# Interleaving the second FFN's up steps with the preceding group's down tiles, and using block products in 15 of its steps instead of 9

## The chip, the cores and the metric

The kernel runs on one core of one Trainium2 chip. The metric is the device time of one execution in microseconds (us). The kernel before was timed three times; its median is 1150.75 us.

## The reference

Two layers of a diffusion transformer work on 512 latent tokens of width 1024 (with 256 context tokens in the first layer). Layer 0 mixes tokens by attention, layer 1 by a Fourier transform, and each ends with a gated feed-forward network (FFN) with a width-3 convolution over the tokens. The change is in the FFN of layer 1 alone. All values are float32.

```python
def conv_ffn(h, w_up, conv_w, conv_b, w_down):     # h 512x1024, w_up 1024x5632, w_down 2816x1024
    u = h @ w_up
    up = jnp.pad(u, ((0, 0), (1, 1), (0, 0)))
    u = up[:, :-2] * conv_w[0] + up[:, 1:-1] * conv_w[1] + up[:, 2:] * conv_w[2] + conv_b
    gate, val = jnp.split(u, 2, axis=-1)
    return (jax.nn.silu(gate) * val) @ w_down

x = x + g1 * rms_norm(y, norm_g[i, 1])
h = modulate(rms_norm(x, norm_g[i, 2]), sh2, sc2)
x = x + g2 * rms_norm(conv_ffn(h, ...), norm_g[i, 3])       # g2 comes from c @ mod_w, a matrix-vector product
```

## The kernel before

Activations lie transposed in SBUF: 128 channels on the partitions, 8 chunks of channels, 512 tokens along the free axis. `xT` is the residual stream (16 KB per partition), `yT` the output of the FFN being summed up, `hh` and `hl` the FFN's input h as a high and a low part.

**Products in three parts.** Each float32 operand is split into a high and a low part, and each product is three matmuls: high by high (L99), high by low (L100), low by high (L101). A weight tile comes by DMA into a ring of three SBUF buffers named `raw` (issued on the queue SP, L131). Then `split` (L122) makes the high part `wh` by a cast on ACT (ScalarE) and the low part `wl` by a subtraction on DVE (VectorE). Both go into rings of five buffers. So each weight tile needs DVE before PE (TensorE) can run the third matmul of its first chunk. A `raw` buffer is free for the next load when the last `split` that reads it is done. Products gather in six PSUM buffers `mm`.

**Up steps.** The FFN has 22 steps, fi = 0 to 21, each for 128 gate channels and 128 value channels. Steps 0 to 2 are begun early, under the norm before the FFN. An ordinary step loads one `raw` of 1 MB (gate and value), splits two weight tiles of 128x1024, and runs 2 x 8 x 3 = 48 matmuls of 128x512. A *block step* (the steps listed in `SEVEN`) takes the same weights as a 2x2 block product by seven products (Strassen's scheme in a variant of Winograd): 7 products x 4 chunks x 3 = 84 matmuls of 128x256 instead of the equivalent of 96. For this, `seven_inputs` forms, once per layer and just ahead of step `SUMS[l]`, four sums of blocks of h on DVE (L1088 to L1091, in place in `yT`) and four more splits (`zh`, `zl`). In every block step `seven_weights` forms three sums of weight blocks on DVE (L1104, L1106, L1107) into a second `raw` buffer, and splits four weight tiles; `seven_products` then runs the seven products, with PSUM copies on ACT and two additions on DVE (L1146, L1149).

**After each step**: the convolution (ACT L1200, DVE L1201 and L1203 for each half), SiLU (ACT L1213), the gating product (DVE L1214), and a split of the gated tile into `xh`, `xl`.

**Groups and down tiles.** The 22 steps are cut into groups of 8, 6 and 8. After a group come 8 *down tiles* d = 0 to 7, one for each 128 output channels. Each loads a slice of w_down, splits it, runs 3 matmuls of 128x512 per step of the group, and copies (first group, ACT) or adds (later groups, DVE L1321) the result to `yT`. After each down tile of the first group, one piece of a matrix-vector product for g2 runs: loads of 1 MB of `in_mod_r` into `raw`, and multiply-adds on DVE (L416, L419). The last group's down tiles run for tokens 0 to 255 first, then `mid` begins the closing norm of that half, then tiles 1 to 7 for tokens 256 to 511 follow.

**What sets the order.** A scheduler places the program's instructions on each engine's list at compile time. It takes, of the instructions whose inputs its own model has ready, the one that stands earliest in the program. On the chip each engine then runs its list strictly in order, and an instruction that waits holds everything behind it. Layer 0 parks `xT` in DRAM (`away`) during its own FFN; layer 1 keeps it in SBUF.

## Time and profile before

| | us |
|---|---|
| median of 3 runs (range) | 1150.75 (1148.4 to 1152.72) |
| profiled execution, its own time | 1151.45 |
| its span in the trace | 1149.7 |
| PE busy | 1117.8 (97%) |
| DVE busy | 877.7 (76%) |
| ACT busy | 578.3 (50%) |
| FFN of layer 1, steps 3 to 7 | 805.5 to 862 |
| its eight first down tiles, with the matrix-vector product | 862 to 907 |
| its nine block steps, each | 10.2 to 10.4 |

The span runs from the first to the last instruction in the trace. Busy time of an engine is an average over stages: DVE's 76% has stretches near 100% in it. A row of a windows view gives, for a stretch of the span, the busy time of PE, PE's weight load, DVE, ACT and POOL, each with its number of instructions, then the granted PE clock (1.00 is full), the DMA engines' busy share and their GB/s. A row of a timeline view gives start, duration, engine, line of the kernel, operation, output and inputs, and in brackets the idle time before it and what ended it.

### The profile page before, as it was taken

To read this page: it belongs to the slowest core of one execution; us is meant where nothing else is said; L and a number is where in the kernel's file an instruction comes from. 1 tells how busy PE (TensorE), PEld (TensorE's weight loads), DVE (VectorE), ACT (ScalarE), POOL (GpSimd) and SP (SyncE) were. 2 spreads that over 40 slices of the span, in tenths; PEclk is the share of its full clock that TensorE was granted. 3 is DMA by queue.
4 is the path that set the end of the run, shared out by engine and by line. 5 is a ranking of instruction groups with operands and counts; after the bars stand their busy time and mean duration, and the time that the engine had idled before them with its cause. 6 is when DMAs were issued, how large, how long until landed. Compare 5 with 4: busy or idle time off the path is not lost.

```text
span 1149.7 us, 19092 instructions
## 1 busy us (share of the span) xinstructions
PE 1117.8 (97%) x7642; PEld 963.9 (84%) x7642; DVE 877.7 (76%) x1422; ACT 578.3 (50%) x1030; POOL 174.0 (15%) x178
## 2 busy tenths in 40 slices
PE   8999999999999999999999998989999999999995
PEld 4689988868888978887998898869887888899895
DVE  4678777765679976987998568988997498679745
ACT  4342356666665633552465445557743355256442
POOL 1236332521420000000000153500000000000023
PEclk9999999999999999999999999999999999999998
DMA  9576101075142355545525300630228123223212
GB/s 366 239 242 214 44 1 38 7 265 205 38 184 111 125 196 198 214 131 201 193 98 191 113 9 15 206 106 35 74 84 281 46 103 111 93 91 111 92 56 74
DMA packets 30881, 149.51 MB, mean 130 GB/s; under 512 B 3140, under 2 KB 7876, under 8 KB 18632
## 3 DMA queue, kind: packets, MB, share of 16 engines
q1 hardware_dynamic: 30792, 148.29, 36.5%
q8 instruction: 60, 0.98, 0.3%
q14 instruction: 29, 0.24, 0.1%
HBM read 144.08 MB, written 4.19 MB: 129 GB/s over the span
## 4 chain that ended last, share of the span: by engine, by line
PE 84%; DVE 8%; ACT 5%; issue 2%; POOL 1%; DMA 0%; DVEq 0%; SPq 0%; ACTq 0%; POOLq 0%
PE mm L99 24%; PE mm L100 23%; PE mm L101 23%; PE PT L914 1%; ACT wh L122 1%; PE mm L174 1%; PE O L99 1%; DVE md_t L291 1%; PE gm L492 1%; PE gm L99 1%; PE O L100 1%; PE gm L101 1%; PE gm L100 1%; PE O L101 1%; PE misc L180 1%
## 5 line engine op out<-in xcount | busy, mean ns | idle before, releaser
L122 ACT CAST wh<-raw 128x1024 fp32r<-128x1024 f32 (+2 forms) x189 | 180.5, 966 | 188.4 <-PE mm L100 128.1
L122 DVE TENSOR_TENSOR wl<-raw,wh 128x1024 fp32r<-128x1024 f32 (+3 forms) x179 | 204.2, 1148 | 63.2 <-ACT wh L122 63.1
L99 PE MATMUL mm<-hh,wh 128*128 128x256 f32 (+2 forms) x652 | 220.8, 339 | 1.4 <-ACT yT L889 0.9
L100 PE MATMUL mm<-hl,wh 128*128 128x256 f32 (+2 forms) x652 | 218.5, 335 | 0.0
L101 PE MATMUL mm<-hh,wl 128*128 128x256 f32 (+2 forms) x652 | 218.4, 335 | 0.0
L266 POOL TENSOR_TENSOR gacc<-gacc,sq 128x256 f32<-128x256 f32 (+1 forms) x35 | 29.9, 855 | 716.0 <-ACT sq L264 715.1
L99 PEld LDWEIGHTS mm<-hh,wh 128*128 128x128 f32 x652 | 122.6, 188 | 18.7 <-ACT sq L1140 2.7
L100 PEld LDWEIGHTS mm<-hl,wh 128*128 128x128 f32 x652 | 122.7, 188 | 14.1
L101 PEld LDWEIGHTS mm<-hh,wl 128*128 128x128 f32 x652 | 122.7, 188 | 14.0
L99 PE MATMUL mm<-xh,wh 128*128 128x512 f32 (+1 forms) x368 | 132.1, 359 | 0.0
L100 PE MATMUL mm<-xl,wh 128*128 128x512 f32 (+1 forms) x368 | 130.9, 356 | 0.0
L101 PE MATMUL mm<-xh,wl 128*128 128x512 f32 (+1 forms) x368 | 130.4, 355 | 0.0
L99 PE MATMUL mm<-zh,wh 128*128 128x256 f32 x304 | 87.0, 286 | 0.0
L100 PE MATMUL mm<-zl,wh 128*128 128x256 f32 x304 | 84.7, 279 | 0.0
L101 PE MATMUL mm<-zh,wl 128*128 128x256 f32 x304 | 84.5, 278 | 0.0
L99 PEld LDWEIGHTS mm<-xh,wh 128*128 128x128 f32 x368 | 69.2, 188 | 12.8 <-issue 2.1
L100 PEld LDWEIGHTS mm<-xl,wh 128*128 128x128 f32 x368 | 69.2, 188 | 11.2 <-issue 0.4
L101 PEld LDWEIGHTS mm<-xh,wl 128*128 128x128 f32 x368 | 69.2, 188 | 10.9
L1200 ACT ACTIVATE cv<-mm,cols 128x512 f32<-128x512 f32 x64 | 49.7, 777 | 26.2 <-PE mm L101 23.3
L99 PEld LDWEIGHTS mm<-zh,wh 128*128 128x128 f32 x304 | 57.2, 188 | 3.5 <-ACT sq L1143 2.7
L101 PEld LDWEIGHTS mm<-zh,wl 128*128 128x128 f32 x304 | 57.3, 188 | 0.0
L1201 DVE SCALAR_TENSOR_TENSOR cv<-mm,cols,cv 128x511 f32<-128x511 f32 x64 | 47.6, 745 | 12.6 <-ACT cv L1200 11.7
(417 smaller groups left out, 2684.8 us busy)
## 6 DMA issues: line engine op xcount, KB each, us to landing
raw<-in_w_up SPq DMA_DIRECT2D x44, 1024.0 KB, 4.9
xT<-in_mod_r SPq DMA_DIRECT2D x20, 1024.0 KB, 5.0
raw<-in_w_down SPq DMA_DIRECT2D x32, 512.0 KB, 3.7
raw<-in_mod_p SPq DMA_DIRECT2D x8, 1024.0 KB, 4.8
raw<-in_w_in SPq DMA_DIRECT2D x6, 1024.0 KB, 7.6
raw<-in_w_down SPq DMA_DIRECT2D x16, 384.0 KB, 3.1
yT<-in_mod_r SPq DMA_DIRECT2D x10, 512.0 KB, 5.9
raw<-in_w_out SPq DMA_DIRECT2D x4, 1024.0 KB, 5.0
```

The lines of the kernel that those rows point to most:

```text
L99: i = PE.matmul(out, lhsT=ah, rhs=bh, start=start, stop=False, skip_group_check=skip)
L100: PE.matmul(out, lhsT=ah, rhs=bl, start=False, stop=False, skip_group_check=skip)
L101: return i, PE.matmul(out, lhsT=al, rhs=bh, start=False, stop=stop, skip_group_check=skip)
L122: i = S.copy(out=h, in_=src), eng.tensor_tensor(out=l, in0=src, in1=f(h), op=ALU.subtract)
L174: PE.matmul(ps[:32, :src.shape[1]], lhsT=ones32, rhs=src, start=True, stop=True)
L180: PE.matmul(ps[32 * j:32 * j + 32, :w], lhsT=ones32, rhs=sq[:, j * w:(j + 1) * w], start=first, stop=last)
L266: G.tensor_tensor(out=self.acc[:, sl], in0=self.acc[:, sl], in1=sq[:, sl], op=ALU.add)
L291: m = V.scalar_tensor_tensor(out=t, in0=yT[:, k, hs], scalar=der[:, l, gi, k:k + 1], in1=R, op0=ALU.mult, op1=ALU.mult)
L492: PE.matmul(ps[32 * q:32 * q + 32, :], lhsT=spad[:, k, :], rhs=w[:, q * T:(q + 1) * T], start=k == 0, stop=k == KC - 1)
L914: PE.transpose(out=pt[:, j * P:(j + 1) * P], in_=Ps[j][:, off:off + P], identity=ident)
L1200: S.activation(out=cv, in_=ps, func=AF.Identity, bias=bc, scale=wc[1])
L1201: V.scalar_tensor_tensor(out=cv[:, 1:], in0=ps[:, :T - 1], scalar=wc[0], in1=cv[:, 1:], op0=ALU.mult, op1=ALU.add)
```

## The change

In layer 1 only:

- the groups become 4, 6, 6, 6 steps; `SUMS` goes from 7 to 6 and `SEVEN` from nine steps to all of 7 to 21;
- the down tiles of a group (all but the last group's) become a generator that is advanced after up steps of the next group, by the table `DOWN`: after step 7 two tiles, after 8 and 9 three each, after 10 to 12 one each, and so on; the matrix-vector product for g2 goes with the tiles of the first group, so with steps 7 to 9;
- `xT` is written to DRAM after the norm ahead of the FFN; its SBUF holds the gated tiles of steps 0 to 3 and 10 to 13; it is loaded back ahead of the last group's down tiles;
- the down weights become one array for each layer and group.

The seven products, the splits and the convolution are as before. Lines move by two to three (L122 becomes L124, L1088 to L1091 become L1090 to L1093, L1104 becomes L1106, L1201 and L1203 become L1204 and L1206, L1214 becomes L1217, L419 becomes L421).

```diff
-GROUPS = [(0, 8), (8, 6), (14, 8)]
+GROUPS = [[(0, 8), (8, 6), (14, 8)], [(0, 4), (4, 6), (10, 6), (16, 6)]]
-SUMS = [5, 7]
-SEVEN = [(5, 6, 8, 10, 12, 14, 15, 17, 18, 20), (8, 9, 11, 12, 14, 15, 17, 18, 20)]
+SUMS = [5, 6]
+SEVEN = [(5, 6, 8, 10, 12, 14, 15, 17, 18, 20), (7, 8, 9, 10, 11, 12, 13, 14, 15, 16, 17, 18, 19, 20, 21)]
+DOWN = {7: 2, 8: 3, 9: 3, 10: 1, 11: 1, 12: 1, 13: 2, 14: 1, 15: 2, 16: 1, 17: 1, 18: 1, 19: 2, 20: 1, 21: 2}
...
-                gs["t"] = xp.pair([P, 2, T])
+                gs["t"] = places.pop(0) if l and (f0 == 0 or f0 == 10 and fi < 14) else xp.pair([P, 2, T])
...
+        def down_part(gi, w, g_, d, hs, ps=None, end=False):
+            ps, sl = y_mm(pps, w, g_, hs, True, ps)
+            if gi == 0:
+                S.copy(out=yT[:, d, sl], in_=ps[:, sl])
+            else:
+                V.tensor_tensor(out=yT[:, d, sl], in0=yT[:, d, sl], in1=ps[:, sl], op=ALU.add)
+            if end:
+                ys.add(pps, yT[:, d, sl], hs)
+
+        def down_weights(gi, nch, d, pairs):
+            r = raw([P, nch, P], a["w_down%d%d" % (l, gi)][d])
+            wh, wl = pairs([P, nch, P])
+            split(wh, wl, r)
+            return [(wh[:, c, :], wl[:, c, :]) for c in range(nch)]
+
+        def down_tiles(gi, nch, g_):
+            yield
+            for d in range(KC):
+                down_part(gi, down_weights(gi, nch, d, wpair), g_, d, [0, 1])
+                pump(gem, GP[1])
+                yield
...
             remod(1, *n2, R[1], eng=V)
+            SY.dma_start(out=away, in_=xT)
+            xp2 = mk(cp, [P, 2, 2, 2, T], F32R, "xT")
+            places = [(xp2[:, i, 0], xp2[:, i, 1]) for i in (0, 1, 0, 1)]
...
-        for gi, (f0, nch) in enumerate(GROUPS):
+        down = iter(())
+        for gi, (f0, nch) in enumerate(GROUPS[l]):
...
                 gated(fi, cc[0], cc[1], f0)
...
+                if l:
+                    pump(down, DOWN.get(fi, 0))
+            pump(down, 100)
+            if l and end:
+                xT = mk(cp, [P, KC, T], F32, "xT")
+                SY.dma_start(out=xT, in_=away)
             g_ = [gs[fi] for fi in range(f0, f0 + nch)]
+            if l and not end:
+                down = down_tiles(gi, nch, g_)
+                pump(down)
+                continue
```

The scheduler's lists move with this. Three places follow; a name's numbers tell one use of a buffer from the next.

**DVE, steps 5 to 7 of layer 1, before.** `wl_1300` is the value half's weights of step 5, `wl_1305` and `wl_1309` the gate's and the value's of step 6, `wl_1324` the gate's of step 7; `cv` is the convolution; L1088 is the first of the four input sums.

```order
L122 TENSOR_TENSOR wl_1300_8961<-raw_1294_8925,wh_1299_8960 128x1024
L1214 TENSOR_TENSOR cv1_1291_8915<-cv0_1287_8882,cv1_1291_8915 128x512
L122 TENSOR_TENSOR wl_1305_9000<-raw_1303_8997,wh_1304_8999 128x1024
L122 TENSOR_TENSOR xl_1293_8922<-cv1_1291_8915,xh_1292_8921 128x512
L1201 SCALAR_TENSOR_TENSOR cv0_1298_8956<-mm_1297_8931,cols_2_64,cv0_1298_8956 128x511
L122 TENSOR_TENSOR wl_1309_9033<-raw_1303_8997,wh_1308_9032 128x1024
L1203 SCALAR_TENSOR_TENSOR cv0_1298_8956<-mm_1297_8931,cols_2_64,cv0_1298_8956 128x511
L1088 TENSOR_TENSOR yT_5_68<-yT_5_68 128x4x256
L122 TENSOR_TENSOR wl_1324_9094<-raw_1322_9091,wh_1323_9093 128x1024
```

The same place in the change, in two pieces of which the second goes on where the first ends. `wl_1297` is the value half's weights of step 5, L1090 and L1091 are the first two input sums.

```order
L124 TENSOR_TENSOR wl_1297_8959<-raw_1291_8923,wh_1296_8958 128x1024
L1217 TENSOR_TENSOR cv1_1288_8913<-cv0_1284_8880,cv1_1288_8913 128x512
L1204 SCALAR_TENSOR_TENSOR cv0_1295_8954<-mm_1294_8929,cols_2_64,cv0_1295_8954 128x511
L1090 TENSOR_TENSOR yT_5_68<-yT_5_68 128x4x256
L124 TENSOR_TENSOR xl_1290_8920<-cv1_1288_8913,xh_1289_8919 128x512
L1206 SCALAR_TENSOR_TENSOR cv0_1295_8954<-mm_1294_8929,cols_2_64,cv0_1295_8954 128x511
```

The rows right behind them: `zl` are the input blocks' low parts, L1092 and L1093 the other two sums, and `wl_1310` is the gate's weights of step 6.

```order
L1091 TENSOR_TENSOR yT_5_68<-yT_5_68 128x4x256
L124 TENSOR_TENSOR zl_1301_9000<-yT_5_68,zh_1300_8999 128x1024
L1204 SCALAR_TENSOR_TENSOR cv1_1299_8987<-mm_1298_8962,cols_2_64,cv1_1299_8987 128x511
L1092 SCALAR_TENSOR_TENSOR yT_5_68<-yT_5_68 128x4x256
L1206 SCALAR_TENSOR_TENSOR cv1_1299_8987<-mm_1298_8962,cols_2_64,cv1_1299_8987 128x511
L1093 SCALAR_TENSOR_TENSOR yT_5_68<-yT_5_68 128x4x256
L1217 TENSOR_TENSOR cv1_1299_8987<-cv0_1295_8954,cv1_1299_8987 128x512
L124 TENSOR_TENSOR zl_1303_9004<-yT_5_68,zh_1302_9003 128x1024
L124 TENSOR_TENSOR xl_1290_8920<-cv1_1299_8987,xh_1289_8919 128x512
L124 TENSOR_TENSOR zl_1305_9008<-yT_5_68,zh_1304_9007 128x1024
L124 TENSOR_TENSOR zl_1307_9012<-yT_5_68,zh_1306_9011 128x1024
L124 TENSOR_TENSOR wl_1310_9018<-raw_1308_9015,wh_1309_9017 128x1024
```

Before, one instruction stands between step 5's value weights and step 6's gate weights; in the change sixteen do, the whole of the input sums and their splits among them.

**PE, from the last matmul of step 5 on, before.** `mm_1301` is step 5's value product, `mm_1306` step 6's gate product.

```order
L101 MATMUL mm_1301_8964<-hh_6_69,wl_1300_8961 128x512
L100 MATMUL mm_1306_9003<-hl_7_70,wh_1304_8999 128x512
L101 MATMUL mm_1306_9003<-hh_6_69,wl_1305_9000 128x512
L99 MATMUL mm_1306_9003<-hh_6_69,wh_1304_8999 128x512
L100 MATMUL mm_1306_9003<-hl_7_70,wh_1304_8999 128x512
```

The same in the change: `mm_1298` is step 5's value product, `mm_1311` and `mm_1315` step 6's gate and value products, `mm_1330` the first product of block step 7.

```order
L103 MATMUL mm_1298_8962<-hh_6_69,wl_1297_8959 128x512
L102 MATMUL mm_1311_9021<-hl_7_70,wh_1309_9017 128x512
L101 MATMUL mm_1315_9054<-hh_6_69,wh_1313_9050 128x512
L102 MATMUL mm_1315_9054<-hl_7_70,wh_1313_9050 128x512
L101 MATMUL mm_1330_9112<-hh_6_69,wh_1321_9095 128x256
L102 MATMUL mm_1330_9112<-hl_7_70,wh_1321_9095 128x256
L103 MATMUL mm_1311_9021<-hh_6_69,wl_1310_9018 128x512
```

Five matmuls that need high parts only stand ahead of the first one that reads `wl_1310`; before, step 6's second matmul already reads its `wl`.

**DVE, the matrix-vector product among the first group's down tiles, before.** L419 works on `raw` tiles loaded from `in_mod_r`; the `wl` here are down weights.

```order
L419 SCALAR_TENSOR_TENSOR gacc_1339_9223<-raw_1341_9232,scol_12_77,gacc_1339_9223 128x1024
L122 TENSOR_TENSOR xl_1313_9068<-cv1_1330_9155,xh_1312_9067 128x512
L122 TENSOR_TENSOR wl_1344_9239<-raw_1342_9236,wh_1343_9238 128x1024
L419 SCALAR_TENSOR_TENSOR gacc_1339_9223<-raw_1346_9268,scol_12_77,gacc_1339_9223 128x1024 x2
L122 TENSOR_TENSOR wl_1349_9275<-raw_1347_9272,wh_1348_9274 128x1024
L419 SCALAR_TENSOR_TENSOR gacc_1339_9223<-raw_1351_9304,scol_12_77,gacc_1339_9223 128x1024 x2
```

Part of it in the change, around the end of block step 8. `wl_1353` and `wl_1355` are the last two weight tiles of block step 8, `wl_1366` and `wl_1371` down weights, L421 the matrix-vector product on `raw_1368`, loaded from `in_mod_r`; L1148 and L1151 are the additions at the end of block step 8.

```order
L124 TENSOR_TENSOR wl_1353_9281<-raw_1347_9268,wh_1352_9280 128x1024
L124 TENSOR_TENSOR xl_1318_9086<-cv1_1334_9209,xh_1317_9085 128x512
L124 TENSOR_TENSOR wl_1355_9285<-raw_1346_9266,wh_1354_9284 128x1024
L124 TENSOR_TENSOR wl_1366_9399<-raw_1364_9396,wh_1365_9398 128x512
L421 SCALAR_TENSOR_TENSOR gacc_1339_9237<-raw_1368_9416,scol_12_77,gacc_1339_9237 128x1024
L1148 TENSOR_TENSOR mm_1356_9288<-mm_1356_9288,sq_1358_9290 128x512
L421 SCALAR_TENSOR_TENSOR gacc_1339_9237<-raw_1368_9416,scol_12_77,gacc_1339_9237 128x1024
L1151 TENSOR_TENSOR mm_1357_9289<-mm_1357_9289,sq_1359_9291 128x512
L1204 SCALAR_TENSOR_TENSOR cv0_1360_9382<-mm_1356_9288,cols_2_64,cv0_1360_9382 128x511
L124 TENSOR_TENSOR wl_1371_9423<-raw_1369_9420,wh_1370_9422 128x512
```

In the lists before, the L419 rows stand between down weights alone, behind all of step 7 and ahead of block step 8's weight sums; now they stand between the splits, additions and convolutions of block steps 7 to 9.

More of the change, by code (lines that the diff above doesn't have):

```diff
@@ L1178, in ffn @@
     def ffn(l, xp, ready, pre, mid, gem, plain=None):
+        nonlocal xT
         ys = YStat()
@@ L1296, in ffn @@
             :, :, NF:], scalar1=-1.0, scalar2=None, op0=ALU.mult)
-        for gi, (f0, nch) in enumerate(GROUPS):
-            end = gi == len(GROUPS) - 1
+        down = iter(())
+        for gi, (f0, nch) in enumerate(GROUPS[l]):
+            end = gi == len(GROUPS[l]) - 1
             for fi in range(max(f0, FIRST), f0 + nch):
@@ L1627, in _layout @@
     out = {}
-    for h, (f0, n) in enumerate(GROUPS):
-        out["w_down%d" % h] = wd[:, f0:f0 + n].transpose(0, 3, 2, 1, 4)
+    for l, groups in enumerate(GROUPS):
+        for g, (f0, n) in enumerate(groups):
+            out["w_down%d%d" % (l, g)] = wd[l, f0:f0 + n].transpose(2, 1, 0, 3)
     wf = i["fourier_w_out"][0].reshape(4, 256, D)
```

13 lines of the change are left out of this document (2 added, 11 removed).

## The prediction

> **What bounds the kernel now.** I read the page's busy shares and its chain of waits first.
>
> ```profile
> PE 1117.8 (97%) x7642; PEld 963.9 (84%) x7642; DVE 877.7 (76%) x1422; ACT 578.3 (50%) x1030; POOL 174.0 (15%) x178
> PE 84%; DVE 8%; ACT 5%; issue 2%; POOL 1%; DMA 0%; DVEq 0%; SPq 0%; ACTq 0%; POOLq 0%
> ```
>
> PE is at work in 97% of the span and carries 84% of the chain that ended last. So work taken off PE saves time one for one, and any idling of PE is lost the same way. What could make PE idle shows only stage by stage, in the windows view of layer 1's FFN (PE, PEld, DVE, ACT, POOL busy, then clock, DMA share, GB/s): steps 3 to 6, step 7 and the tail of 6, then the first group's down tiles.
>
> ```profile
> core 0: us, PE busy (x) PEld busy (x) DVE busy (x) ACT busy (x) POOL busy (x), PEclk, DMA share, GB/s
> 790.00:833.40 43.40, 43.23 (x248) 37.62 (x247) 41.60 (x86) 35.76 (x63) 0.00 (x0) 1.00 0.14 49
> 833.40:856.80 23.40, 23.40 (x103) 18.97 (x102) 22.25 (x26) 12.56 (x17) 0.00 (x0) 1.00 0.14 46
> 862.00:907.00 45.00, 45.00 (x201) 35.59 (x200) 28.82 (x30) 15.13 (x20) 0.00 (x0) 1.00 0.57 197
> ```
>
> PE is full in all three. But DVE is full as well from 790 to 857 (41.60 of 43.40 us, then 22.25 of 23.40): there it just keeps up, and nothing can be put in front of it unseen. Only in the down tiles has it air (28.82 of 45). This decides the forecast: the change spends DVE's time earlier.
>
> **The saving.** A block step against an ordinary one, by the stretches that each occupies on PE:
>
> ```profile
> 907.19:917.61 10.42, 10.42 (x86) 10.10 (x85) 3.11 (x4) 5.18 (x8) 0.00 (x0) 1.00 0.08 34
> 917.61:928.01 10.40, 10.33 (x87) 9.94 (x86) 10.13 (x14) 7.10 (x12) 0.00 (x0) 1.00 0.53 185
> 928.01:939.21 11.20, 11.20 (x51) 9.01 (x50) 10.97 (x16) 6.43 (x10) 0.00 (x0) 1.00 0.04 17
> ```
>
> The first two are block steps, the third an ordinary one of 11.20 us (48 matmuls, 0.233 us each). The nine block steps' stretches, cut like these, have a mean of 10.35 us. Six more of them save 6 x (11.20 - 10.35) = **5.1 us**.
>
> **A stall at step 6.** On DVE's list the change puts all of the input sums and their splits between step 5's last weights and step 6's first. What these cost, from the DVE timeline of before, start to start:
>
> ```profile
> 832.27 1.22 DVE L122 TENSOR_TENSOR wl<-raw,wh 128x1024 fp32r<-128x1024 f32 x1
> 833.40 0.68 DVE L1214 TENSOR_TENSOR cv<-cv,cv 128x512 f32<-128x512 f32 x1
> 834.00 1.22 DVE L122 TENSOR_TENSOR wl<-raw,wh 128x1024 fp32r<-128x1024 f32 x1
> ...
> 838.17 0.74 DVE L1203 SCALAR_TENSOR_TENSOR cv<-mm,cols,cv 128x511 f32<-128x511 f32 x1
> 838.83 1.21 DVE L1088 TENSOR_TENSOR yT<-yT 128x1024 f32<-128x1024 f32 x1
> 839.96 1.22 DVE L122 TENSOR_TENSOR wl<-raw,wh 128x1024 fp32r<-128x1024 f32 x1
> ...
> 843.55 1.21 DVE L1090 SCALAR_TENSOR_TENSOR yT<-yT 128x1024 f32<-128x1024 f32 x1
> 844.68 0.68 DVE L1214 TENSOR_TENSOR cv<-cv,cv 128x512 f32<-128x512 f32 x1
> ```
>
> So 1.13 us for anything 1024 wide (split or sum), 0.60 for a gating product or a split 512 wide, 0.66 for a tap of the convolution. The row at 832.27 is step 5's value weights; the row at 834.00 is step 6's gate weights, on time. In the change 17 instructions run from 833.40 up to and with `wl_1310`: nine of 1024 (four sums, four `zl`, itself), 10.2 us; four of 512, 2.4; four taps, 2.6; together 15.2 us. Waits on the way: the second of them needs step 5's gate product and its pass through ACT, about 0.6 us; the taps of step 5's value half wait some 0.3 for theirs. So `wl_1310` is ready near 833.4 + 15.2 + 0.9 = 849.5.
>
> PE's side, from its timeline:
>
> ```profile
> 805.54 0.50 PE L99 MATMUL mm<-hh,wh 128*128 128x512 f32 x1 [0.17 <-DVE sq L1199]
> ```
>
> This is the start of step 3. Three steps of 11.20 end at 839.1. The five matmuls that PE's list has ahead of the first use of `wl_1310` take 3 x 0.233 + 2 x 0.118 = 0.9, so PE stands at 840.1 and idles until 849.5: **9.4 us**. It is a plain loss: PE's work behind it is not shorter, and DVE's load is not less. Bounds: with no wait on DVE's side 8.5; if the value half's chain through ACT is as slow as the one which costs 0.55 more at the `xl` split between those rows, twice, 10.5.
>
> **The clock after it.** The trace has one such gap, at the end of the Fourier stage:
>
> ```profile
> 752.00:756.40 4.40, 1.06 (x18) 0.69 (x20) 3.90 (x5) 1.71 (x5) 1.47 (x1) 1.00 0.80 257
> 756.40:759.80 3.40, 3.40 (x46) 2.21 (x47) 1.70 (x7) 1.18 (x5) 0.00 (x0) 0.50 0.73 284
> 759.80:770.00 10.20, 9.59 (x89) 6.64 (x88) 9.61 (x28) 6.03 (x16) 0.00 (x0) 1.00 0.01 2
> ```
>
> PE worked 1.06 of 4.40 us, then had half its clock (0.50) for 3.4 us although it was busy throughout, then all of it. A gap of 9.4 us brings the same at least: half of 3.4 us lost, **1.7 us**; bounds 0 and 3.4 (twice the row).
>
> [...]
>
> **Steps 7 to 9 with tiles and the matrix-vector product.** Here a ring of three `raw` buffers has to hold a block step's weights, its sums, down weights, and four loads of `in_mod_r`. Landing times and the DVE work on them:
>
> ```profile
> raw<-in_w_up SPq DMA_DIRECT2D x44, 1024.0 KB, 4.9
> raw<-in_mod_r SPq DMA_DIRECT2D x4, 1024.0 KB, 5.0
> raw<-in_w_down SPq DMA_DIRECT2D x16, 384.0 KB, 3.1
> ...
> 861.80 0.75 DVE L416 TENSOR_SCALAR gacc<-raw,scol 128x1024 f32<-128x1024 f32 x1 [0.67 <-DMA raw<-in_mod_r]
> 862.60 1.28 DVE L419 SCALAR_TENSOR_TENSOR gacc<-raw,scol,gacc 128x1024 f32<-128x1024 f32 x1
> ```
>
> In the change `raw_1368` takes the buffer of block step 8's weights, which the last split of that step, `wl_1355`, frees; one down split (0.6) behind it stands L421 on `raw_1368`. So DVE waits 5.0 - 0.6 = 4.4 us for that load, with the additions and taps of step 8, the down weights and step 9's weights queued behind it. The same happens a step earlier, where two taps and a down split cover part of it: about 3 us. Two losses of DVE, 7.4 us, against the air that the down tiles give: steps 7 to 9 hold 3 x 10.35 + 8 x 2.8 = 53.5 us of PE work (a down tile of four steps is 12 x 0.233 = 2.8). DVE's work in that time: the sums and splits of steps 8, 9 and 10, each 4 x 1.13 + 3 x 0.60 = 6.3, 18.9 in all; the endings of steps 6 to 9 (four taps, gating, `xl`: 3.8, and two additions of 0.60 after a block step: 5.0), 18.9; eight rows of the matrix-vector product, 0.8 + 7 x 1.3 = 9.9; eight down splits, 4.8; together 52.5. With 7.4 of waits 59.9, 6.4 more than PE's 53.5. DVE enters the stretch ahead of PE by its early work on step 7 (about 5 us), but can use this only where its list's order lets it. I take **3.5 us**, bounds 0 (the waits fall under PE's backlog of tiles) and 7.4 (none does).
>
> **Steps 10 to 21.** A period with one down tile of six steps takes PE 10.35 + 4.2 = 14.55 us, the 4.2 from the eight such tiles of before:
>
> ```profile
> 971.06:1004.65 33.59, 33.59 (x145) 27.07 (x144) 20.41 (x25) 8.30 (x10) 0.00 (x0) 1.00 0.23 78
> ```
>
> In such a period the next step's weights come into the same `raw` buffer that this step's leave (ring of three: weights, sums, down weights). From the weights' landing to their last split DVE's list has four instructions 1024 wide, six 512 wide and one tap, 8.8 us; with the load's 4.9 a loop of 13.7, under 14.55 by 0.85. I take 0; at a load of 6.9 us (the slowest kind below) each of the eight one-tile periods would be 1.25 longer, +10.
>
> **x in DRAM and the tail.** Layer 0 does the same once, and its rows give the price:
>
> ```profile
> away<-xT SPq DMA_DIRECT2D x1, 2048.0 KB, 6.9
> xT<-away SPq DMA_DIRECT2D x1, 2048.0 KB, 8.2
> ...
> 774.91 0.33 SPq L131 DMA_DIRECT2D raw<-in_w_up  x1
> ...
> 807.35 0.33 SPq L131 DMA_DIRECT2D raw<-in_w_up  x1
> ...
> 782.88 0.42 DVE L293 TENSOR_TENSOR xT<-xT,md_t 128x256 f32<-128x256 f32 x1
> ```
>
> SP issues nothing between 774.91 and 807.35, and the last update of `xT` starts at 782.88; the store lands near 790, before any gated tile is written (step 0's convolution follows the start of step 3 at 805.5). Cost 0. The reload's 8.2 us and the down weights queued behind it on SP lie under step 21, two tiles and the last group's first tiles; I take 0, and up to +2 where it is late. In the closing stretch the half sweep of seven tiles falls from 21.2 us (24 matmuls each) to 7 x 18 x 0.118 = 14.9; what it must cover is the closing norm of the first half, which starts with DVE's L291 and is over before the next rows:
>
> ```profile
> 1121.58 0.88 DVE L291 SCALAR_TENSOR_TENSOR md_t<-yT,der,Rs 128x256 f32<-128x256 f32 x2 [1.20 <-ACT Rs L215]
> 1127.54 1.07 DVE L1321 TENSOR_TENSOR yT<-yT,mm 128x256 f32<-128x256 f32 x3
> ```
>
> The sweep began at 1115.3, so 12.2 us cover it, and 14.9 are there. Cost 0, at most 0.5.
>
> **Sum.** -5.1 + 9.4 + 1.7 + 3.5 = +9.5. The profiled execution took 1151.45 us, 0.7 above the median; against the median the forecast is 1150.75 + 9.5 = **1160.3 us**.
>
> **Rivals.**
>
> *DVE keeps up at step 6.* Then the whole saving arrives and the rest costs nothing: 1145.7. For it: before, DVE also did these sums and splits among ordinary steps, and PE lost nothing. Against: there step 6's and 7's weights stood in front of them on the list, and now they stand behind. It decides by the time of `wl_1310`: with it ready before 840.1 + 5.1 = 845.2 the kernel would not be slower. Chance 0.08.
>
> *Only the first stall counts*; the `in_mod_r` waits vanish under the tiles: -5.1 + 9.4 + 1.7 = +6.0, 1156.8. For it: 45 us with 28.82 of DVE's before. Chance 0.18.
>
> *The raw ring fails in steps 10 to 21*, by the slower load: +10 on the forecast, 1170.3. For it: the loop has only 0.85 us of air. Against: `in_w_up` lands in 4.9. Chance 0.11.
>
> *Block steps save nothing among tiles*: the PSUM copies queue on ACT behind the casts of down weights, and a step takes 11.2 again: +5.1 on the forecast, 1165.4. Against: ACT has 7.10 of 10.40 us in a full block step. Chance 0.07.
>
> The forecast itself: 0.56.
>
> **How the numbers follow.** The likeliest is 1160.3. A change of under 0.5% (5.75 us, about what a measurement here can tell from none) reaches up to 1156.5: that takes the first rival and half of the second, and a little of the forecast at its lower bounds. Faster than 1145.0 needs the saving and more; 0.04. Same 0.14, slower 0.82. The range from 1151 to 1170.5 leaves out the first rival and half of the third, and the upper mishaps in pairs; the forecast's own bounds are 1154 to 1167.
>
> **What would show it.** In the trace after: PE idle for 8 to 10 us just before the first L103 on step 6's gate, its releaser DVE's `wl`, behind L1093 and four splits; right after it a clock of 0.50 for 3.4 us or more; DVE waiting for `in_mod_r` at L418 or L421 for 3 to 4 us, twice; block steps of 10.2 to 10.4 throughout; no waits for `raw` from step 10 on. A PE without a gap near 840, or a gap of under 5 us, would make the forecast wrong; so would a DVE that idles in the periods from step 10 on.

## The result and the profile after

The changed kernel took 1160.13 us (median of 5 runs, 1157.45 to 1161.99), the kernel before 1151.4 beside it (5 runs, 1148.4 to 1153.32): a ratio of 1.0078, 95% interval 1.0058 to 1.0098. It is slower by 8.7 us; the forecast was +9.5, to 1160.3.

The page of the profiled execution (1157.57 us, span 1155.8), busy shares and chain:

```profile
PE 1113.4 (96%) x7816; PEld 968.8 (84%) x7816; DVE 912.7 (79%) x1480; ACT 598.8 (52%) x1074; POOL 173.8 (15%) x178
PE 79%; DVE 12%; ACT 4%; issue 2%; DMA 2%; POOL 1%; DVEq 0%; SPq 0%; ACTq 0%; POOLq 0%
```

PE is busy for 4.4 us less (the block steps), in a span that is 6.1 us longer, and DVE's share of the chain that ended last has gone from 8% to 12%. PE's timeline shows where:

```profile
802.94 0.50 PE L101 MATMUL mm<-hh,wh 128*128 128x512 f32 x1 [0.16 <-DVE sq L1202]
...
837.55 0.27 PE L102 MATMUL mm<-hl,wh 128*128 128x256 f32 x1
847.21 0.79 PE L103 MATMUL mm<-hh,wl 128*128 128x512 f32 x1 [9.38 <-DVE wl L124]
847.80 0.63 PE L101 MATMUL mm<-hh,wh 128*128 128x512 f32 x1
...
877.66 0.39 PE L103 MATMUL mm<-zh,wl 128*128 128x256 f32 x1 [0.29 <-DVE wl L124]
893.26 0.64 PE L435 MATMUL misc<-gacc,ones 128*32 128x256 f32 x8 [0.81 <-DVE gacc L421]
894.45 0.39 PE L101 MATMUL mm<-hh,wh 128*128 128x256 f32 x1 [0.56 <-ACT wh L124]
...
1143.41 0.70 PE L197 MATMUL misc<-gacc,ones 128*128 128x256 f32 x2 [0.49 <-POOL gacc L268]
```

Step 3 starts at 802.94; behind five matmuls that need only high parts, of which the one at 837.55 is the last, PE idles for 9.38 us, until DVE has made the low part of step 6's gate weights. DVE's timeline over the same time:

```profile
829.22 1.22 DVE L124 TENSOR_TENSOR wl<-raw,wh 128x1024 fp32r<-128x1024 f32 x1
830.35 0.69 DVE L1217 TENSOR_TENSOR cv<-cv,cv 128x512 f32<-128x512 f32 x1
831.94 0.75 DVE L1204 SCALAR_TENSOR_TENSOR cv<-mm,cols,cv 128x511 f32<-128x511 f32 x1 [0.90 <-ACT cv L1203]
...
837.74 0.75 DVE L1204 SCALAR_TENSOR_TENSOR cv<-mm,cols,cv 128x511 f32<-128x511 f32 x1 [0.39 <-ACT cv L1203]
...
843.67 2.35 DVE L124 TENSOR_TENSOR zl<-yT,zh 128x1024 fp32r<-128x1024 f32 x2
845.94 2.35 DVE L124 TENSOR_TENSOR wl<-raw,wh 128x1024 fp32r<-128x1024 f32 x2
```

The row at 829.22 is step 5's value weights, the first of the two at 845.94 step 6's gate weights: done 16.7 us after the other, with 1.3 of waits in it. The last input splits stand directly ahead of it. What PE's clock did then, by windows:

```profile
837.83:847.21 9.38, 0.00 (x1) 0.00 (x1) 9.38 (x11) 3.56 (x4) 0.00 (x0) 0.72 0.00 0
847.21:852.20 4.99, 4.99 (x12) 3.93 (x13) 4.99 (x6) 1.04 (x1) 0.00 (x0) 0.51 0.21 54
852.20:860.00 7.80, 7.80 (x36) 6.33 (x35) 4.03 (x5) 3.66 (x5) 0.00 (x0) 1.00 0.45 168
...
915.83:926.19 10.36, 10.35 (x85) 9.96 (x84) 7.83 (x10) 5.14 (x9) 0.00 (x0) 1.00 0.38 139
944.72:954.95 10.23, 10.23 (x85) 9.96 (x84) 8.77 (x14) 5.68 (x9) 0.00 (x0) 1.00 0.29 108
```

DVE worked throughout the gap (9.38 of 9.38 us). Then PE had half its clock for the first 4.9 us: twelve matmuls took 5.1 us instead of 12 x 0.233 = 2.8, a loss of 2.3. The last two rows are block steps 10 and 12: among tiles they cost what they did before. For the matrix-vector product, DVE waited as follows (in all, times, longest):

```profile
DVE gacc L421 <- DMA raw<-in_mod_r: 3.1, 2, 2.5
```

For the comparisons below I use the *FFN stretch*: from step 3's first matmul to PE's closing product on `gacc`. It was 1136.53 - 805.54 = 331.0 us before and is 1143.41 - 802.94 = 340.5 now: +9.5. Behind it the kernel is 0.8 shorter. Ahead of it, in stages that the change leaves as they were, this execution is 2.6 us shorter. By 21 us it is already 2.2 ahead (the same ACT row starts at 21.14 before and at 18.99 here), and the rest comes and goes with the half clock: before, it fell for 3.4 us each at 8.9, 691.5 and 756.4, here for 6.8 us at 722.4. In the Fourier stage's gap, where it fell before, it did not:

```profile
755.30:758.70 3.40, 3.15 (x50) 1.50 (x50) 2.61 (x11) 1.38 (x6) 0.00 (x0) 1.00 0.70 287
```

So the spans differ by 9.5 - 0.8 - 2.6 = 6.1, the medians by 8.7. Over all profiled executions here step 3 starts anywhere from 801.7 to 807.7 us, which is about as much as single times of one kernel spread (5 us). So the FFN stretch, which leaves this out, is a useful second measure beside the medians. It is the stretch of one execution, and the half clock in it varies too (last section).

### The profile page after: what moved, and what is told of

Read it like the earlier page. It is cut to its first block, busy times and chain, and to the rows that moved or that the text cites. A ratio compares the mean times of both kernels' runs of the same rounds, so it can differ in the third digit from the quotient of the medians.

```text
span 1155.8 us, 19581 instructions
## 1 busy us (share of the span) xinstructions
PE 1113.4 (96%) x7816; PEld 968.8 (84%) x7816; DVE 912.7 (79%) x1480; ACT 598.8 (52%) x1074; POOL 173.8 (15%) x178
## 4 chain that ended last, share of the span: by engine, by line
PE 79%; DVE 12%; ACT 4%; issue 2%; DMA 2%; POOL 1%; DVEq 0%; SPq 0%; ACTq 0%; POOLq 0%
PE mm L101 22%; PE mm L103 21%; PE mm L102 21%; DVE wl L124 2%; PE PT L916 1%; DVE md_t L293 1%; PE O L101 1%; PE gm L494 1%; ACT wh L124 1%; PE gm L101 1%; PE O L102 1%; PE gm L103 1%; PE gm L102 1%; PE O L103 1%; PE mm L176 1%
## 5 line engine op out<-in xcount | busy, mean ns | idle before, releaser
L124 ACT CAST wh<-raw 128x1024 fp32r<-128x1024 f32 (+2 forms) x209 | 192.6, 932 | 173.3 <-PE mm L102 107.1
L124 DVE TENSOR_TENSOR wl<-raw,wh 128x1024 fp32r<-128x1024 f32 (+2 forms) x199 | 216.9, 1098 | 57.8 <-ACT wh L124 57.3
L101 PE MATMUL mm<-zh,wh 128*128 128x256 f32 x400 | 113.9, 285 | 0.0
L103 PE MATMUL mm<-zh,wl 128*128 128x256 f32 x400 | 111.3, 278 | 0.5 <-DVE wl L124 0.5
L102 PE MATMUL mm<-zl,wh 128*128 128x256 f32 x400 | 111.5, 279 | 0.0
L101 PE MATMUL mm<-xh,wh 128*128 128x512 f32 (+1 forms) x302 | 107.4, 356 | 0.0
L102 PE MATMUL mm<-xl,wh 128*128 128x512 f32 (+1 forms) x302 | 106.9, 354 | 0.0
L103 PE MATMUL mm<-xh,wl 128*128 128x512 f32 (+1 forms) x302 | 106.3, 352 | 0.0
L101 PEld LDWEIGHTS mm<-zh,wh 128*128 128x128 f32 x400 | 75.4, 189 | 4.0 <-ACT sq L1145 3.4
L102 PEld LDWEIGHTS mm<-zl,wh 128*128 128x128 f32 x400 | 75.2, 188 | 0.0
L1229 DVE TENSOR_TENSOR yT<-yT,mm 128x256 f32<-128x256 f32 (+1 forms) x54 | 28.8, 543 | 34.0 <-PE mm L103 33.9
```

The source lines that it names most:

```text
L101: i = PE.matmul(out, lhsT=ah, rhs=bh, start=start, stop=False, skip_group_check=skip)
L102: PE.matmul(out, lhsT=ah, rhs=bl, start=False, stop=False, skip_group_check=skip)
L103: return i, PE.matmul(out, lhsT=al, rhs=bh, start=False, stop=stop, skip_group_check=skip)
L124: i = S.copy(out=h, in_=src), eng.tensor_tensor(out=l, in0=src, in1=f(h), op=ALU.subtract)
L1229: V.tensor_tensor(out=yT[:, d, sl], in0=yT[:, d, sl], in1=ps[:, sl], op=ALU.add)
```

## The experiments

The theory: two losses, both from DVE's list and the ring behind it (the gap at step 6 with its half clock, and the matrix-vector product among block steps), outweigh 5 us of saved PE work. The rivals: interleaving costs by itself; block steps do; the gap has another source than DVE's list; x in DRAM is not hidden. Each experiment changes the changed kernel, except the eighth. All twelve variants beside each other ("before" is the median of the runs of the kernel before on the same chips):

| kernel | median us | before | ratio, 95% interval | FFN stretch | PE's waits, step 3 to 21 (us) |
|---|---|---|---|---|---|
| before | 1151.4 | | | 331.0 | 0.2 |
| the change | 1160.13 | 1151.4 | 1.0078 (1.0058 to 1.0098) | 340.5 | 11.5 |
| 1 sums ahead of step 7 | 1161.35 | 1150.04 | 1.0093 (1.0075 to 1.0111) | 340.9 | 9.9 |
| 2 input splits on POOL | 1163.18 | 1150.04 | 1.0111 (1.0091 to 1.0131) | 342.6 | 10.8 |
| 3 no matrix-vector product | 1156.84 | 1150.04 | 1.0062 (1.0044 to 1.008) | 337.6 | 8.6 |
| 4 interleaving, nine block steps | 1157.26 | 1150.04 | 1.0066 (1.0047 to 1.0084) | 338.4 | 5.2 |
| 5 fourteen, product late | 1157.16 | 1151.44 | 1.0065 (1.0041 to 1.0088) | 337.2 | 7.0 |
| 6 nine, product late | 1151.81 | 1151.44 | 1.0009 (0.9995 to 1.0022) | 331.9 | 0.2 |
| 7 change, product late | 1168.71 | 1151.44 | 1.0161 (1.0138 to 1.0183) | 348.2 | 15.6 |
| 8 block steps alone | 1174.23 | 1151.44 | 1.0203 (1.0176 to 1.023) | 350.9 | 19.7 |
| 9 blocks from 10 | 1153.75 | 1150.41 | 1.0019 (1.0005 to 1.0034) | 332.6 | 2.3 |
| 10 blocks from 9 | 1154.26 | 1150.41 | 1.0032 (1.002 to 1.0043) | 335.2 | 5.5 |
| 11 x twice | 1161.95 | 1150.41 | 1.0096 (1.0075 to 1.0117) | 341.9 | 11.4 |
| 12 ten, product late | 1151.88 | 1149.81 | 1.0017 (1.0003 to 1.0031) | 331.4 | 0.2 |

### 1 The sums one step later

```diff
-SUMS = [5, 6]
+SUMS = [5, 7]
```

> The changed kernel with the input sums and their splits put ahead of step 7 instead of step 6 (SUMS 7). Nothing else differs. Theory A, the gap at step 6 comes from the place of this work on DVE's list: step 6's weights now stand ahead of it, so PE runs step 6 without a gap. The work itself (10.2 us of DVE) is still more than DVE has to spare by block step 7, whose first weights by the list are ready 5 to 6 us after PE gets there. PE's largest gap goes from 9.4 to about 5 us and moves to step 7; time about 1154 to 1156. Rival B, the length of the gap is set by DVE's whole backlog wherever it stands: a gap of 9 us at step 7, time about 1160.

PE's timeline, all rows with a wait between 850 and 880:

```profile
856.84 0.58 PE L101 MATMUL mm<-zh,wh 128*128 128x256 f32 x1 [5.48 <-ACT wh L124]
875.77 0.39 PE L101 MATMUL mm<-hh,wh 128*128 128x256 f32 x1 [1.48 <-ACT wh L124]
877.46 0.58 PE L101 MATMUL mm<-zh,wh 128*128 128x256 f32 x1 [1.18 <-ACT wh L124]
```

The first wait ends with ACT's cast of the weight sums, which DVE has only just made (L1106 stands behind the input splits on its list). The gap moved with the sums, to block step 7, and is 5.48 us: the place on the list makes it, as theory A had it. But the time did not fall. New gaps of 1.48 and 1.18 us stand at block step 8, and behind them the clock was halved a second time:

```profile
877.23:880.65 3.42, 3.19 (x13) 2.84 (x13) 3.42 (x6) 1.97 (x4) 0.00 (x0) 0.50 0.00 0
```

DVE's waits say where the new gaps come from:

```profile
DVE gacc L421 <- DMA raw<-in_mod_r: 3.2, 1, 3.2
DVE gacc L418 <- DMA raw<-in_mod_r: 3.1, 1, 3.1
```

In the change PE's idling lets DVE, and the loads that wait for buffers which DVE frees, run ahead of it: the first load of `in_mod_r` is issued 51.8 us after step 3's start (at 854.74), here 54.8 (at 861.08). Here DVE waits 6.3 us for these loads, in the change 3.1, and PE pays for it. The two losses are not independent, as my sum had them.

### 2 The input splits on POOL

```diff
-    def seven_inputs(xp):
+    def seven_inputs(xp, eng=V):
...
-            split(*b[n], src)
+            split(*b[n], src, eng)
...
-                    bs = seven_inputs(xp)
+                    bs = seven_inputs(xp, G if l else V)
```

> The changed kernel with the four low-part splits of layer 1's input sums on POOL, which has nothing to do in this stage, instead of DVE. Theory A (DVE's list is late): 4 x 1.13 = 4.5 us less ahead of step 6's weights on that list, and by the new list only two of the four sums are still ahead of them, so they are ready about when PE gets there: gap under 1 us, no half clock, time about 1149 to 1151. Rival B, the gap is set by something that this leaves alone (the load of step 6's weights, or the casts on ACT): the gap stays at 9 us, time about 1160. Rival C, POOL is too slow: by its 128x512 splits (1.3 us) one of 128x1024 is about 2.7 us, four are 10.8, and if they take longer block step 7 waits for the last of them; time 1153 to 1156.

None of the three. POOL's timeline, then DVE's, then PE's waits at step 6:

```profile
839.77 3.48 POOL L124 TENSOR_TENSOR zl<-yT,zh 128x1024 fp32r<-128x1024 f32 x1 [83.23 <-ACT zh L124]
847.28 8.96 POOL L124 TENSOR_TENSOR zl<-yT,zh 128x1024 fp32r<-128x1024 f32 x3 [4.04 <-ACT zh L124]
```

```profile
840.92 3.41 DVE L124 TENSOR_TENSOR wl<-raw,wh 128x1024 fp32r<-128x1024 f32 x1
...
847.84 2.88 DVE L1217 TENSOR_TENSOR cv<-cv,cv 128x512 f32<-128x512 f32 x1
850.64 3.37 DVE L124 TENSOR_TENSOR wl<-raw,wh 128x1024 fp32r<-128x1024 f32 x1
853.93 2.86 DVE L124 TENSOR_TENSOR xl<-cv,xh 128x512 fp32r<-128x512 f32 x1
```

```profile
844.38 0.50 PE L103 MATMUL mm<-hh,wl 128*128 128x512 f32 x1 [1.77 <-DVE wl L124]
854.07 0.80 PE L103 MATMUL mm<-hh,wl 128*128 128x512 f32 x1 [4.29 <-DVE wl L124]
```

While POOL splits, DVE's splits of 1.22 us last 3.4 and its instructions of 0.68 last 2.9; the first of these four DVE rows ends at 844.33 and the POOL row beside it at 843.25, the last at 856.79 and the three POOL splits beside it at 856.24. The four splits taken off DVE's list were worth 4.5 us, and the four slow rows together last 8.7 us longer than they do alone. So POOL's splits cost DVE more time than they took off its list, a rival that my expectation lacked; what makes DVE's rows longer beside POOL's, the runs do not show. PE's waits at step 6 fell from 9.4 to 6.1 us, but waits of 1.4 and 1.2 us and a second half clock came at block step 8, as in the first experiment, and the stretch is 2.1 us longer than the change's.

### 3 Without the matrix-vector product

```diff
-                if not places:
-                    load()
+                if not places:
+                    if kk == 0:
+                        held(V.memset(acc, 0.0))
+                    yield
+                    continue
```

> The changed kernel without the matrix-vector product for g2 among the first tiles: its four loads and eight multiply-adds are left out (g2 is computed from zeros). Theory A (those loads and rows cost PE about 1.9 us in steps 8 and 9): the gap at step 6 is unchanged at 9.4 us, PE idles no more between step 7 and step 10; time 2 us less, about 1158. Rival B, these small gaps come from the block steps following one another: they stay, time 1160.

PE's waits from 800 to 1105:

```profile
PE mm L103 <- DVE wl L124: 7.9, 1, 7.9
PE misc L448 <- ACT gacc L441: 0.5, 1, 0.5
PE mm L101 <- DVE sq L1205: 0.2, 1, 0.2
```

Only the one gap is left (its first part is filled by the product's closing matmuls, which now come earlier), and steps 7 to 21 run without a wait. The stretch is 2.9 us shorter, of which the small gaps of the change are 1.9 and the rest a shorter gap (8.4 us in its two parts) and less half clock. Theory A holds for the small gaps; the gap at step 6 was not quite unchanged.

### 4 The interleaving with nine block steps

```diff
-SUMS = [5, 6]
+SUMS = [5, 7]
-SEVEN = [..., (7, 8, 9, 10, 11, 12, 13, 14, 15, 16, 17, 18, 19, 20, 21)]
+SEVEN = [..., (8, 9, 11, 12, 14, 15, 17, 18, 20)]
```

> The interleaving alone: the changed kernel with the nine block steps of before (8, 9, 11, 12, 14, 15, 17, 18, 20) and the sums ahead of step 7, as before. Theory A (the loss is in the order of DVE's work at step 6 and not in the interleaving): no gap at step 6 or 7 above 1 us, the waits for the matrix-vector product at steps 8 and 9 of about 2 us; time 1151 to 1154. Rival B, groups of 4 and tiles among the steps cost by themselves (tile weights and raw buffers): gaps in steps 7 to 21 of more than 5 us together, time above 1156.

Neither fits whole. There is no gap at step 6 or 7, as theory A said, but steps 8 and 9 cost more than its 2 us: the stretch is 7.4 over the one before, and waits and time are those of rival B. Whether the tiles or the product make them, this run cannot tell. Of PE's 5.2 us of waits from step 3 to 21, 4.8 lie between 865 and 892. The windows view shows them; experiment 6, in which the product alone is elsewhere, has the same window:

```profile
845.00:900.00 55.00, 50.13 (x298) 42.33 (x297) 45.85 (x57) 25.69 (x42) 0.00 (x0) 1.00 0.44 156
```

### 5 to 7 The matrix-vector product late

All three take the product's pieces from the first tiles and put one load each after steps 13, 15, 19 and 21, which two tiles follow:

```diff
-                pump(gem, GP[1])
                 yield
...
                     pump(down, DOWN.get(fi, 0))
+                    if fi in (13, 15, 19, 21):
+                        pump(gem)
```

The sixth has the nine block steps of the fourth; the fifth has 8 to 21 (14), the sums ahead of step 7, and tiles 3, 3, 2 after steps 7, 8, 9; the seventh is the change with this edit alone.

> The interleaving alone with nine block steps, and the matrix-vector product moved to after steps 13, 15, 19 and 21. Against the same kernel with the product at steps 7 to 9 (1157). Theory A: the product's loads and rows were the loss there, about 6 us of gaps at steps 8 and 9; without them time 1150 to 1152. Rival B, the tiles' own weights cost it: gaps stay at steps 8 and 9, time 1156 to 1158.

```profile
845.00:900.00 55.00, 54.87 (x318) 47.65 (x317) 44.26 (x57) 31.75 (x49) 0.00 (x0) 1.00 0.33 113
```

In the same 55 us PE works 54.87 instead of 50.13, and the time is that of the kernel before (ratio 1.0009). This settles two rivals: groups of 4 and 6, tiles among up steps, and x in DRAM cost nothing that the times can show, and 0.9 us in the stretch (331.9 against 331.0), where PE waits 0.45 and 0.54 us in the closing norm; the product's loads at steps 8 and 9 cost about 6 us when no gap has gone before (338.4 against 331.9).

> The changed kernel with three moves: the sums ahead of step 7 and step 7 an ordinary step, as before (14 block steps, 8 to 21); three tiles after step 7 and two after step 9; and the matrix-vector product one load at a time in the periods that hold two tiles (after steps 13, 15, 19 and 21). Theory A (the two losses are DVE's late lists at the sums and at the matrix-vector product, and nothing else in the interleaving costs): no gap above 1 us from step 3 on; five block steps more than before save 5 x 0.85 = 4.3 us, the last stage costs about 1 more than before; time 2 to 4 us under before, 1147 to 1149. Rival B, the ring of three raw buffers cannot take the matrix-vector product's loads among block steps anywhere: gaps of 2 us or more at each of the four places, time 1155 or more.

> The changed kernel with only the matrix-vector product moved to after steps 13, 15, 19 and 21; sums ahead of step 6 as in the change. Theory A: the gap at step 6 and its half clock stay (8 to 9.5 us and 1.5 to 2.5), the gaps at steps 8 and 9 go, no new ones come; time about 1157, as without the product altogether. Rival B, the product costs the same wherever it stands: 1160.

Both went wrong. The fifth's time is that of its rival, with smaller gaps (the largest 2.1, 1.5 and 1.1 us); the seventh lost its gaps at steps 8 and 9, as its theory A said, but gained later ones and is far slower than either forecast. The windows of the fifth, up to step 13 and from there to the last group:

```profile
802.00:985.00 183.00, 182.71 (x1090) 160.23 (x1090) 159.01 (x219) 106.62 (x161) 0.00 (x0) 1.00 0.29 99
985.00:1105.00 120.00, 113.23 (x739) 100.21 (x739) 98.17 (x127) 57.03 (x89) 0.00 (x0) 1.00 0.34 122
```

Until the first load of the product comes, PE loses 0.3 us in 183, with block steps 8 to 12 in a row and the sums ahead of the ordinary step 7. After it PE idles 6.8 in 120. DVE's waits there:

```profile
DVE raw L1106 <- DMA raw<-in_w_up: 11.5, 4, 3.3
...
DVE gacc L421 <- DMA raw<-in_mod_r: 1.9, 1, 1.9
```

A block step's weights come late (11.5 us in four waits), and this in the periods behind a load of the product: its first rows on DVE are at 985.5 and 987.6, the late weights at 1005.8, 1022.8 and 1038.3. So one more load sets the loop back, and with the 0.85 us that I found it to have to spare it does not catch up for three periods. Whether the buffer that the load holds does this, or the 2.6 us of its rows on DVE, is not separated here. With nine block steps (experiment 6) the same loads cost nothing. In the seventh, where steps 7 to 21 are all block steps, the stretch is 10.6 us longer than without the product (experiment 3), 7.0 of it in PE's waits; at steps 7 to 9 the product costs 2.9.

### 8 The block steps alone

The kernel before, with:

```diff
-SUMS = [5, 7]
-SEVEN = [..., (8, 9, 11, 12, 14, 15, 17, 18, 20)]
+SUMS = [5, 6]
+SEVEN = [..., (7, 8, 9, 10, 11, 12, 13, 14, 15, 16, 17, 18, 19, 20, 21)]
```

> The block steps alone: the kernel before, its groups of 8, 6 and 8 and its tiles behind them, with the sums ahead of step 6 and block steps 7 to 21. Theory A: the gap at step 6 comes with the order of the sums and is there without any interleaving, 9 us and 2 of half clock; and block steps in a row are bound by DVE (6.3 of sums and splits and 5.0 of additions, taps and gating, 11.4 us against PE's 10.35), so that PE loses about 1 us in each of the 12 that follow another; time 1150 - 5 + 11 + 12, about 1168. Rival B, DVE keeps up between block steps: no gaps after step 7, about 1156.

PE's waits from 800 to 1106, and the windows of steps 8 to 13 and 14 to 21:

```profile
PE mm L101 <- DVE wl L122: 15.3, 6, 9.4
PE mm L99 <- ACT sq L1143: 1.8, 5, 0.5
```

```profile
916.28:983.57 67.29, 62.97 (x505) 60.22 (x504) 57.79 (x75) 41.52 (x68) 0.00 (x0) 1.00 0.25 82
1017.53:1105.00 87.47, 81.59 (x643) 77.90 (x642) 77.92 (x101) 53.80 (x88) 0.00 (x0) 0.98 0.24 87
```

The gap at step 6 is here too, 9.4 us without any interleaving. And six block steps in a row take 67.3 us instead of 6 x 10.35 = 62.1. PE idles 4.3 and 5.9 us in the two windows, near the 12 that I expected. The second window also holds a half clock of 3.4 us (last section). With tiles among them, steps 10 to 21 of the change ran without a wait: the tiles are what lets block steps in a row run at PE's pace, and the change is right in this part.

### 9, 10 and 12 Looking for a faster version

```diff
-SUMS = [5, 6]
+SUMS = [5, 7]
-SEVEN = [..., (7, 8, 9, 10, 11, 12, 13, 14, 15, 16, 17, 18, 19, 20, 21)]
+SEVEN = [..., (10, 11, 12, 13, 14, 15, 16, 17, 18, 19, 20, 21)]
```

The ninth is this; the tenth begins at step 9 with tiles 3, 4, 1 after steps 7, 8, 9; the twelfth is the sixth with step 10 added.

> The changed kernel with the sums ahead of step 7 and block steps from 10 on (12 of them): steps 7 to 9, which hold the first tiles and the matrix-vector product, are ordinary. Theory A (DVE's load decides where block steps pay: an ordinary step asks 6 us of it, a block step 11.4): no gap above 1 us anywhere; three block steps more than before save 2.6, the last stage costs about 1; time 1 to 2 us under before, 1149 to 1151. Rival B, the matrix-vector product's loads collide with the tiles' weights in the ring of three whatever the steps are: gaps of 3 us or more at steps 7 to 9, time 1153 or more.

> As the run with block steps from 10, with block steps from 9 on (13), and the first group's tiles drawn forward (three after step 7, four after 8, one after 9), so that the matrix-vector product ends within steps 7 and 8. Theory A: no gap above 1 us; 3.4 saved, 1 lost in the last stage; time 2 to 3 us under before, 1148 to 1150. Rival B: step 9's weights are late behind the product's last rows, a gap of 2 to 4 us there, time 1151 to 1153.

> The run with nine block steps and the matrix-vector product after steps 13, 15, 19 and 21, with step 10 a block step as well (ten: 8 to 12, 14, 15, 17, 18, 20). Theory A (with one tile between, block steps in a row cost PE nothing as long as no load of the product stands among them; 14 of them lost nothing from 8 to 12 in the other run): the FFN's stretch from step 3 to PE's last product is 0.85 us shorter than with nine, 332.2 to 331.4, and no gap over 0.5 us comes ahead of the last group; time 1150 to 1152, which a measurement cannot tell from before. Rival B, a third block step in a row brings DVE behind: a gap at steps 11 to 13, the stretch longer than 332.2.

The ninth and tenth went to the side of their rivals, the ninth with a smaller gap than 3 us, the tenth with its gap at step 8 instead of 9. In the ninth one wait of 1.64 us stands at step 8, an ordinary step, and in the tenth one of 2.70 there; the rows of PE's timelines:

```profile
865.27 0.50 PE L101 MATMUL mm<-hh,wh 128*128 128x512 f32 x1 [1.64 <-ACT wh L124]
```

```profile
875.58 0.50 PE L101 MATMUL mm<-hh,wh 128*128 128x512 f32 x1 [2.70 <-ACT wh L124]
```

In the ninth the load of step 8's weights was issued 1.3 us behind one of `in_mod_r` (857.25 and 855.92 on SP's timeline); it landed at 864.15, and ACT cast it at 864.17. Its three more block steps save 2.6 us and the stretch is 1.6 over the one before; that its median is 3.3 over, and not 1.6, I cannot place (the profiled execution took 1148.59 us, 5.2 less than the median). The twelfth went as theory A said: the stretch is 0.55 us under the sixth's (331.4 against 331.9; the expectation, which counts it 0.3 us further, had 0.85), with no wait up to step 21 but 0.2 at step 3. Its time is 1.0017 of the kernel before's (1.0003 to 1.0031). None of these versions beats the kernel before.

### 11 x written and loaded twice

```diff
             SY.dma_start(out=away, in_=xT)
+            SY.dma_start(out=away, in_=xT)
...
                 SY.dma_start(out=xT, in_=away)
+                SY.dma_start(out=xT, in_=away)
```

> The changed kernel with x written to DRAM twice and loaded back twice. Theory A (both are hidden): the second store (6.9 us) falls into SP's free time before step 5's weights, the second load delays the last group's weights by less than their slack; time 1160 as without, at most 2 more. Rival B, the last group's weights already come only just in time: PE waits for about the second load's 6 to 8 us, time 1166 to 1168.

1161.95 against 1160.13, and 1.5 us in the stretch, with 1.2 more of waits among the last group's tiles. The half clock behind the gap took 3.0 us of PE's work here instead of 4.9, which is worth 1.0, so the transfers may cost up to 2.5. Two more of 2 MB, some 15 us of DMA (6.8 for a store and 7.9 for a load in this run), cost that little. So a single store and a single reload are hidden, or nearly.

## Why the prediction was right

Its steps in its own order. Its +9.5 was for the whole time, where +8.7 was measured between the medians; the terms are compared in the FFN stretch, which grew by 9.5:

- **The saving**, 5.1: right. Block steps 10 to 21 took 10.33 us on average (two are shown above). Ten ordinary and nine block steps before (from step 3 on) against four and 15 now come to 5.4.
- **The stall at step 6**, 9.4: measured 9.38. Counted from step 3, PE came to the gap 0.3 us later than worked out, and so did DVE's weights, whose list had 1.3 us of waits where I had 0.9. The order of DVE's list and five prices from rows of the kernel before were enough. Experiments 1 and 8 show that the place of the sums makes it and that interleaving does not; experiments 4 to 6, with the sums ahead of an ordinary step 7, have no such gap. Why the scheduler puts the next step's weights among the sums there, and behind all of them in the change, was not tested.
- **The clock**, 1.7 with bounds 0 and 3.4: measured 2.3, too low by 0.6. I took the 3.4 us of one row for the length of the half clock; here it lasted 10.24 us, 5.3 of them inside the gap and 4.9 on PE's work (last section). Nor was the row the only one: the profile before has two more half clocks of 3.4 us, at 8.9 and 691.5. The upper bound of 3.4, twice the row, held.
- **The matrix-vector product among steps 7 to 9**, 3.5 with bounds 0 and 7.4: measured 1.9 as PE's gaps; without the product the stretch is 2.9 shorter (experiment 3). DVE did wait twice for `in_mod_r`, but 3.1 us together where I had 7.4. The step that was off: I took the two losses as a sum. The gap at step 6 lets loads and DVE run ahead, and covers part of the second loss; without it (experiment 4) the second loss is about 6.
- **Steps 10 to 21**, 0: right, no gap of 0.3 us. By one of its own signs the forecast would have been wrong there: DVE idles 30.6 us between 905 and 1106, 24.7 of them for ACT's casts of weights, which wait for PE (38.4 us in 38 waits). The sign was ill chosen: PE set the pace there, and no wait of DVE's held it. That the loop was nearly closed was right: one more load in it (experiments 5 and 7) and it fails, though by a load more and not by a slower one, as the third rival had it. (A load of 6.9 us would have made a period 6.9 - 4.9 - 0.85 = 1.15 longer and not 1.25, so that rival's +10 should be 9.)
- **x in DRAM and the tail**, 0 with bounds to 2.5: the last group's stage lost about 1 (PE waits 0.36 and 0.49 us in the closing norm, together more than the 0.5 that I gave it), and the end behind it gained 0.8, which no term had. Right in the sum.
- **The first rival** (DVE keeps up) fell with the 9.38; the fourth (block steps cost as ordinary ones) with the 10.33.

Put together, -5.4 + 9.4 + 2.3 + 1.9 + 1 = 9.2, and 0.3 of the stretch's 9.5 stays unplaced. The errors of single terms (the product 1.6 too high, the clock 0.6 and the last stage 1 too low) cancel, and the half clock behind the same gap took between 1.5 us (experiment 11) and 2.8 (experiment 7) elsewhere. So the closeness of the total is part luck; the gap itself is not.

## What to carry to other kernels

A block of work that is inserted into an engine's list in program order goes ahead of what the next engine waits for; if that engine's list is full in the windows there, what the next engine cannot fill with other work becomes a gap (here 9.4 us at step 6, 5.5 one step later), whatever the average share says (DVE had 76%). Losses on one list are one backlog: taking away the first shows the next (experiment 1), so price them together, and look for the ring of buffers behind them. Before work is moved to an engine that idles, see whether the two can run at once (beside POOL's splits, DVE's of 1.22 us took 3.4).
